# Seven block products of 512 columns for the output product, and another order at four joints of a trunk layer

## The chip, the cores and the metric

One NeuronCore of one Trainium2 chip runs the whole layer in one launch. The metric is the device time of an execution in microseconds (us); of several runs the median counts. The engines are named as in the profile: PE (TensorE, matmuls; PEld its weight loads), DVE (VectorE), ACT (ScalarE), POOL (GpSimd), SP (SyncE, which here only issues DMAs).

## What is computed

One layer of a decoder trunk with 512 tokens of 2048 channels, and 256 memory tokens. The input is normalised and projected onto 17408 columns: queries, keys, values and gates of three branches (block-sparse attention A with 8 heads, dilated windows B with 3 groups of 4 heads, cross-attention M into the memory with 4 heads) and three merge gates of 2048 columns.

```python
def reference(x, mem, norm_in_g, norm_mem_g, w_in, w_mem_kv, w_proj_a, w_proj_b, w_proj_m, w_out, norm_final_g):
    mem_n = rms_norm(mem, norm_mem_g)
    h = rms_norm(x, norm_in_g[layer])
    proj = jnp.einsum('bsd,de->bse', h, w_in[layer])
    (qa, ka, va, za, qb, kb, vb, zb, qm, zm, gates) = jnp.split(proj, split_points, axis=-1)
    ...
    mkv = jnp.einsum('bmd,de->bme', mem_n, w_mem_kv[layer])
    mk, mv = jnp.split(mkv, 2, axis=-1)
    ...
    g_a, g_b, g_m = jnp.split(jax.nn.sigmoid(gates), N_BRANCH, axis=-1)
    merged = (g_a * jnp.einsum('bse,ed->bsd', ya, w_proj_a[layer])
              + g_b * jnp.einsum('bse,ed->bsd', yb, w_proj_b[layer])
              + g_m * jnp.einsum('bse,ed->bsd', ym, w_proj_m[layer]))
    x = x + jnp.einsum('bsd,de->bse', merged, w_out[layer])
    return rms_norm(x, norm_final_g)
```

Everything is in float32 outside. Inside, each operand of a large product is cut into two parts, hi (rounded) and lo (the rest), and a product is three matmuls: hi x hi, hi x lo, lo x hi. ACT makes hi, DVE then lo = raw - hi. Each cut thus costs one instruction on either engine, and PE waits for both.

## The kernel before

Every engine takes its instructions in the order in which they stand in its queue; the order comes from the order of the code (a scheduler adds the semaphores). Weights come as pieces of 128 x 1024 through SP's queue; `load_half` (L67 to 79) cuts one into `whi` and `wlo`, of which three buffers each are kept. Four PSUM banks are called `acc`, four `att`.

- **Start, 5.9 to 79.6 us.** The first six columns of the gate path Z of branch M, with matmuls 512 tokens wide. Meanwhile `Rows.cut` (`mrows`) cuts the memory rows into `thi`, `tlo`, adding the squares on POOL (L207), and `normalize` (L275) scales the rows of x.
- **Memory keys, 79.6 to 136 us** (the loop over `h` and `c`, L320 to 330). Eight units K0 to K7, each a `project` of 16 x 3 matmuls of 256 columns (L97 to 99), which needs two cuts of weights; DVE then takes `mk` out of the bank (L327). After each two units `forms(h)` makes the forms of one pair of rows of x: sums and differences of the four 256-column blocks (L301 to 304), each then split into hi and lo (L149, L150): `u` (both T1 and T2), `halft` (T3), and the rows themselves into `kept`.
- **Memory values, 136 to 179.5 us.** `product_rows` (L102) with matmuls of 512 columns (L117 to 119); ACT takes `mv` out (L124). Four more forms are made here, two after each half.
- **Input products, from 179.5 us on.** A `Pair` of two 128-column units is computed by seven block products instead of eight (`steps`, L392 on; matmuls L360 to 362 of 256 columns) with weight sums on DVE (L397, L402, L415). Between them stand the attention of the branches, and `project_branch` (L598), the projection of a branch (its results leave from 375 to 450 us for M, 834 to 908 for A, 1358 to 1398 for B), which first splits all rows y of the branch. A list `later` holds small jobs, of which `run` pops one after each step.
- **The class table** of branch B's masks (`cls`, L713 to 719) is made on POOL at 909.6 us, transposed by PE (L717) and read back as `rowc`.
- **Gates, to 1839.8 us.** Eight triples of pairs; `projected` rows are loaded again (`pj`, through SP's queue) and DVE makes `merged` (L880, L882). Twelve of sixteen merged rows are spilled to DRAM and come back as `mg`.
- **Output product, 1839.8 to 2014.1 us.** `product_out` (L905 to 907): four column blocks of 512, four token blocks, 16 row blocks, three matmuls of 512 columns each. `cut_out` cuts the weights (`shi`, `slo`, L149, L150), DVE adds the residual (L924), ACT squares, POOL multiplies by the final gain (L928).
- **End, 2014.1 to 2023.1 us.** Scale of the last rows and stores.

`split` is in all of these places the same two instructions:

```python
nc.scalar.activation(hi, t, AF.Copy)
nc.vector.tensor_tensor(lo, t, hi.bitcast(F32), op=OP.subtract)
```

## Time and profile before

| | us |
|---|---|
| three runs | 2023.8, 2024.47, 2024.96 |
| median | 2024.47 |
| the profiled execution | 2024.92 |
| its span, first to last instruction | 2023.1 |
| PE busy | 1989.4 (98%) |
| DVE busy | 1466.7 (72%) |
| ACT busy | 988.0 (49%) |
| POOL busy | 124.1 (6%) |

The busy time of an engine counts every moment in which one of its instructions is under way; matmuls overlap, so the mean length of one is longer than the spacing of two. Windows give these per stretch, together with PEclk, the granted clock of PE (1.00 is 2.4 GHz, 0.50 is 1.2 GHz). A wait names the instruction that stood, and the one that released it. In the timeline, instructions of the same kind in a row are one line; the next start is the end of their spacing.

### The profile page before, as it was taken

How to read it: one execution, taken by the hardware profiler on the slowest of the kernel's cores; microseconds unless marked ns; L12 is line 12 of the kernel's file. 1: busy time of each engine (PE TensorE's matmuls, PEld its weight loads, DVE VectorE, ACT ScalarE, POOL GpSimd, SP SyncE). 2: the span in 40 equal slices, each digit the busy share in tenths (PEclk: the TensorE clock that was granted, in tenths of full speed). 3: DMA queues.
4: the chain of work that ended last, by engine and by line, in shares of the span. 5: the costliest groups of instructions: out<-in, count | busy, mean ns of one | idle time of the engine just before them, and what ended most of it. 6: DMA issues, size and time to landing. Idle time of an engine off the chain costs nothing.

```text
span 2023.1 us, 34915 instructions
## 1 busy us (share of the span) xinstructions
PE 1989.4 (98%) x14337; PEld 1886.9 (93%) x14337; DVE 1466.7 (72%) x1844; ACT 988.0 (49%) x1556; POOL 124.1 (6%) x179
## 2 busy tenths in 40 slices
PE   8999999999999999899999999999999999999998
PEld 6898999889999999789999999998999999998886
DVE  7977778338888888437887979855787878786233
ACT  6545565336555555323646454554444444445223
POOL 4200010010000000010000000001000000000110
PEclk9899999999999999999999999999999999999999
DMA  7464344433223223333322332345444444437332
GB/s 236 160 204 156 114 137 143 149 110 110 91 98 105 98 96 129 132 125 101 89 99 95 109 94 87 113 132 183 138 144 140 143 142 129 162 120 270 105 104 83
DMA packets 87600, 261.87 MB, mean 129 GB/s; under 512 B 15504, under 2 KB 16528, under 8 KB 87440
## 3 DMA queue, kind: packets, MB, share of 16 engines
q1 hardware_dynamic: 77376, 227.12, 33.9%
q0 software_dynamic: 9920, 32.51, 4.7%
q8 instruction: 112, 1.84, 0.4%
q14 instruction: 48, 0.39, 0.1%
q10 hardware_dynamic: 144, 0.02, 0.0%
HBM read 232.31 MB, written 27.30 MB: 128 GB/s over the span
## 4 chain that ended last, share of the span: by engine, by line
PE 54%; POOL 0%; ACT 0%; DVE 0%; ACTq 0%; issue 0%
PE acc L362 14%; PE acc L361 14%; PE acc L360 14%; PE acc L906 3%; PE acc L905 3%; PE acc L907 3%; PE acc L98 1%; PE acc L97 1%; PE acc L99 1%; PE att L822 1%; PE att L757 0%; PE att L811 0%; PE att L621 0%; PE att L762 0%; POOL combs L711 0%; PE att L760 0%
## 5 line engine op out<-in xcount | busy, mean ns | idle before, releaser
L350 ACT ACTIVATE whi<-raw 128x1024 fp32r<-128x1024 f32 x455 | 482.6, 1061 | 591.6 <-PE acc L361 396.1
L351 DVE TENSOR_TENSOR wlo<-raw,whi 128x1024 fp32r<-128x1024 f32 x455 | 555.8, 1222 | 199.2 <-ACT whi L350 189.0
L360 PE MATMUL acc<-kept,whi 128*128 128x256 f32 x2080 | 591.2, 284 | 0.6 <-ACT whi L350 0.3
L361 PE MATMUL acc<-kept,whi 128*128 128x256 f32 x2080 | 589.4, 283 | 0.4 <-DVE kept L150 0.4
L362 PE MATMUL acc<-kept,wlo 128*128 128x256 f32 x2080 | 589.1, 283 | 0.0
L360 PEld LDWEIGHTS acc<-kept,whi 128*128 128x128 f32 x2080 | 399.3, 192 | 1.6 <-ACT kept L149 0.7
L361 PEld LDWEIGHTS acc<-kept,whi 128*128 128x128 f32 x2080 | 399.5, 192 | 1.1 <-DVE kept L150 0.8
L362 PEld LDWEIGHTS acc<-kept,wlo 128*128 128x128 f32 x2080 | 399.3, 192 | 0.0
L360 PE MATMUL acc<-shi,whi 128*128 128x256 f32 x1040 | 296.7, 285 | 2.5 <-ACT shi L149 2.0
L361 PE MATMUL acc<-slo,whi 128*128 128x256 f32 x1040 | 296.4, 285 | 0.4 <-DVE slo L150 0.4
L362 PE MATMUL acc<-shi,wlo 128*128 128x256 f32 x1040 | 296.4, 285 | 0.0
L360 PEld LDWEIGHTS acc<-shi,whi 128*128 128x128 f32 x1040 | 201.5, 194 | 3.4 <-ACT shi L149 2.2
L361 PEld LDWEIGHTS acc<-slo,whi 128*128 128x128 f32 x1040 | 201.3, 194 | 1.0 <-DVE slo L150 0.6
L362 PEld LDWEIGHTS acc<-shi,wlo 128*128 128x128 f32 x1040 | 201.3, 194 | 0.2 <-DVE wlo L351 0.2
L78 DVE TENSOR_TENSOR wlo<-raw,whi 128x1024 fp32r<-128x1024 f32 x78 | 96.5, 1237 | 143.2 <-ACT whi L77 139.2
L77 ACT ACTIVATE whi<-raw 128x1024 fp32r<-128x1024 f32 x78 | 82.6, 1059 | 168.5 <-PE acc L98 126.1
L360 PE MATMUL acc<-T,whi 128*128 128x256 f32 x520 | 147.4, 283 | 0.0
L362 PE MATMUL acc<-T,wlo 128*128 128x256 f32 x520 | 147.2, 283 | 0.0
L361 PE MATMUL acc<-T,whi 128*128 128x256 f32 x520 | 147.2, 283 | 0.0
L98 PE MATMUL acc<-slo,whi 128*128 128x512 f32 x320 | 125.1, 391 | 4.3 <-DVE slo L150 4.3
L99 PE MATMUL acc<-shi,wlo 128*128 128x512 f32 x320 | 124.8, 391 | 0.0
L97 PE MATMUL acc<-shi,whi 128*128 128x512 f32 x320 | 121.4, 392 | 1.8 <-ACT shi L149 1.8
(244 smaller groups left out, 3199.3 us busy)
## 6 DMA issues: line engine op xcount, KB each, us to landing
raw<-in_w_in SPq DMA_DIRECT2D x266, 512.0 KB, 3.7
raw<-in_w_mem SPq DMA_DIRECT2D x32, 512.0 KB, 4.4
raw<-in_w_out SPq DMA_DIRECT2D x32, 512.0 KB, 6.1
projected<-pr POOLq DMA_DIRECT2D x48, 256.0 KB, 2.6
pj<-projected SPq DMA_DIRECT2D x48, 256.0 KB, 5.5
raw<-in_w_pm SPq DMA_DIRECT2D x16, 512.0 KB, 4.0
raw<-in_w_pa SPq DMA_DIRECT2D x16, 512.0 KB, 4.3
traw<-in_xT SPq DMA_DIRECT2D x16, 256.0 KB, 5.9
```

What stands on the lines that cost most here:

```text
L77: nc.scalar.activation(hi, raw, AF.Copy)
L78: nc.vector.tensor_tensor(lo, raw, hi.bitcast(F32), op=OP.subtract)
L97: nc.tensor.matmul(ps, whi, hi[i], start=i == 0, stop=False)
L98: nc.tensor.matmul(ps, whi, lo[i], start=False, stop=False)
L99: nc.tensor.matmul(ps, wlo, hi[i], start=False, stop=i == n - 1)
L350: nc.scalar.activation(hi, raw, AF.Copy)
L351: nc.vector.tensor_tensor(lo, raw, hi.bitcast(F32), op=OP.subtract)
L360: nc.tensor.matmul(ps, hi[:, sl], f[0], start=start and k == 0, stop=False, skip_group_check=True)
L361: nc.tensor.matmul(ps, hi[:, sl], f[1], start=False, stop=False, skip_group_check=True)
L362: nc.tensor.matmul(ps, lo[:, sl], f[0], start=False, stop=stop and k == 7, skip_group_check=True)
L905: nc.tensor.matmul(b, hi[:, sl], whi, start=k == 0, stop=False)
L906: nc.tensor.matmul(b, hi[:, sl], wlo, start=False, stop=False)
```

## The change

1. **Output product by seven block products.** Tokens are halved (2 x 256), the 2048 inputs are halved (8 row pairs), and two column blocks of 512 make a column pair. Per column pair seven products (forms B11, T1, T2, B21, T3, B22, T4 of the merged rows with sums of weight pieces) of four pieces each with 12 matmuls of 512 columns. `prepare` cuts a piece (`parts_1024`, `wlo` at L375 of the changed kernel) and makes its sums (`add_to`, L953).
2. **Forms of the merged rows** are made in the gate stage (`merged_forms`), T1 and T2 kept on the chip, the others spilled to `waiting` and fetched through POOL's queue by jobs in `later`. `pj` and the residual rows come through POOL's queue too.
3. **Order.** The class table's transpose moves to the start. The memory rows are cut before `silu_rows`. `forms` is called after each key unit but the first, and once in the middle of the values. The splits of y go to `later` before a projection. `turn_b` comes after `flush`.
4. **Memory.** 25 instead of 49 tiles of 512 columns (`slot`), 18 instead of 6 of 1024 (`raw`); T1/T2, T3 and the rows of x lie in the latter.

```diff
-SLOTS = 49
-RAWS = 6
+SLOTS = 25
+RAWS = 18
@@ at the start
+    clsT = att_bank()
+    nc.tensor.transpose(clsT[:, :P], classes(), ident)
+    rowc = sb.tile([P, 1], F32, name="rowc")
+    nc.vector.tensor_copy(rowc, clsT[:, 0:1])
@@ first units
-    for c in range(8):
+    for c in range(4):
         mrows.load()
     for i in range(EARLY):
         if i >= FIRST:
             first.append(project(w_in[U_ZM + i], hT))
-        nc.gpsimd.dma_start(zdram[i], silu_rows(first[i]))
-        if i >= FIRST:
             for c in range(3 if i < EARLY - 1 else 2):
                 mrows.cut()
+                if len(mrows.raw) < 8:
+                    mrows.load()
             for k in range(*((0, 5), (5, 11), (11, NK))[i - FIRST]):
                 normalize(k)
+        nc.gpsimd.dma_start(zdram[i], silu_rows(first[i]))
@@ memory keys and values
             nc.vector.tensor_tensor(t[:, c * MEM:(c + 1) * MEM], ps, mrow, op=OP.mult)
+            if h or c:
+                forms(2 * h + c - 1)
         nc.gpsimd.dma_start(mkd[h], t)
-        forms(h)
     for g in range(2):
...
-        forms(4 + 2 * g)
-        forms(5 + 2 * g)
+        if g == 0:
+            forms(7)
@@ Pair.run
-                if next(self.todo, None) and later:
-                    later.pop(0)()
+                at = next(self.todo, None)
+                if at:
+                    for _ in range(-(-len(later) // (8 - at))):
+                        later.pop(0)()
@@ before each project_branch, and in it
+    def act_later(y):
+        parts, tiles = [], [f() for f in y[:2]]
+        def one():
+            n = len(parts)
+            if n + 2 < len(y):
+                tiles.append(y[n + 2]())
+            parts.append(split(tiles[n]))
+        later.extend([one] * len(y))
+        return parts
...
-        act = tuple(zip(*[split(t()) for t in y]))
+        act = tuple(zip(*y))
...
+            if later:
+                later.pop(0)()
@@ gates
-                pr = slot("pj")
-                nc.sync.dma_start(pr, projected[b * NK + dt])
+            prs = [fetched(projected[b * NK + dt], "pj") for dt in pair]
...
+        merged_forms(i)
@@ output product, per column pair cp
+    def prepare(n):
+        if n < len(work) and n not in ready:
+            f, i = work[n]
+            raw = f(i)
+            raw, after = raw if isinstance(raw, tuple) else (raw, None)
+            if n < len(work) - 4:
+                ready[n] = parts_1024(raw)
+            else:
+                ready[n] = split(raw, (wide_tile("last", F32R), wide_tile("last", F32R)))
+            if after:
+                after()
+
+    def multiply(banks, n, form, start, stop, tiles=(0, 1), pieces=range(4)):
+        for i in pieces:
+            prepare(n + i + 1)
+            if n + i < len(work) - 8:
+                prepare(n + i + 2)
+            hi, lo = ready[n + i]
+            for t in tiles:
+                for kk in range(2):
+                    f = M[form][2 * i + kk]
+                    fh, fl = (p[:, t * P:(t + 1) * P] for p in f)
+                    wh, wl = (p[:, kk * 512:(kk + 1) * 512] for p in (hi, lo))
...
+                    nc.tensor.matmul(banks[t], fh, wh, start=first, stop=False, skip_group_check=True)
+                    nc.tensor.matmul(banks[t], fh, wl, start=False, stop=False, skip_group_check=True)
+                    nc.tensor.matmul(banks[t], fl, wh, start=False, stop=last, skip_group_check=True)
+            if later:
+                later.pop(0)()
...
+        multiply(xs, n, "B11", True, False)
+        for t in range(2):
+            add_block(t, c1, xs[t], OP.add)
+            residual(2 + t, c2)
+        multiply(ys, n + 4, "T1", True, False)
...
+        multiply(xs, n + 8, "T2", False, False)
...
+        multiply(zs, n + 12, "B21", True, True)
+        for t in range(2):
+            add_block(t, c1, zs[t], OP.add)
+            gained(t, c1)
...
+        multiply(xs, n + 16, "T3", False, False)
...
+        multiply(ys, n + 20, "B22", False, True)
...
+            multiply(xs, n + 24, "T4", False, True)
```

What the change does to the queues is seen best in the order of the instructions. First DVE's queue in the memory keys, around the end of K2, before (`slo`, `T`, `kept` are lo parts of the forms):

```order
L78 TENSOR_TENSOR wlo<-raw,whi 128x1024
L327 TENSOR_TENSOR mk<-acc,mrow 128x256
L301 TENSOR_TENSOR u<-traw 128x256
L78 TENSOR_TENSOR wlo<-raw,whi 128x1024
L303 SCALAR_TENSOR_TENSOR u<-u,traw 128x256
L304 SCALAR_TENSOR_TENSOR traw<-u,traw 128x256
L78 TENSOR_TENSOR wlo<-raw,whi 128x1024
L150 TENSOR_TENSOR slo<-u,shi 128x512
L150 TENSOR_TENSOR T_1070<-halft,T_1070 128x256
L327 TENSOR_TENSOR mk<-acc,mrow 128x256
L150 TENSOR_TENSOR kept_75<-traw,kept_75 128x512
L78 TENSOR_TENSOR wlo<-raw,whi 128x1024
```

And in the changed kernel, from the weights of K3 and K4 to those of K5 and K6:

```order
L91 TENSOR_TENSOR wlo<-raw,whi 128x1024 x4
L350 TENSOR_TENSOR mk<-acc,mrow 128x256 x2
L321 TENSOR_TENSOR u<-xraw 128x256 x2
L323 SCALAR_TENSOR_TENSOR u<-u,xraw 128x256 x2
L324 SCALAR_TENSOR_TENSOR xraw<-u,xraw 128x256 x2
L163 TENSOR_TENSOR T_1157<-u,T_1157 128x512
L163 TENSOR_TENSOR kept_83<-xraw,kept_83 128x512
L163 TENSOR_TENSOR kept_84<-xraw,kept_84 128x512
L163 TENSOR_TENSOR T_1234<-u,T_1234 128x512
L163 TENSOR_TENSOR T_1237<-halft,T_1237 128x256 x2
L91 TENSOR_TENSOR wlo<-raw,whi 128x1024 x4
```

Each `mk` reads the bank of its unit, as before (the two of `x2` are those of K3 and K4); the instructions of two forms now stand between the second `mk` and the next `wlo`, those of K5, in one block, where before a few stood between single `wlo`, and one `wlo` of the next unit or two stood ahead of each `mk`.

The second place is ACT's queue in the memory values, where the first half ends, before:

```order
L149 ACTIVATE kept_77<-traw 128x512
L77 ACTIVATE whi<-raw 128x1024 x8
L124 ACTIVATE mv<-acc,mcol 128x512
L77 ACTIVATE whi<-raw 128x1024
L124 ACTIVATE mv<-acc,mcol 128x512
L77 ACTIVATE whi<-raw 128x1024
L149 ACTIVATE shi<-u 128x512
```

And changed:

```order
L162 ACTIVATE T_1391<-u 128x512
L162 ACTIVATE T_1394<-halft 128x256 x2
L90 ACTIVATE whi<-raw 128x1024 x10
L137 ACTIVATE mv<-acc,mcol 128x512 x2
L162 ACTIVATE T_1560<-u 128x512
L162 ACTIVATE kept_87<-xraw 128x512
L90 ACTIVATE whi<-raw 128x1024 x8
```

The second `mv` had a `whi` ahead of and behind it; now two hi parts stand between it and the next eight `whi`.

The third place is DVE's queue in the output product. Before, from the last merged rows on, all cuts of a column block stand in a row (`x16`, 512 columns):

```order
L150 TENSOR_TENSOR kept_86<-mg,kept_86 128x512
L150 TENSOR_TENSOR kept_87<-mg,kept_87 128x512
L924 TENSOR_TENSOR res<-acc,res 128x512 x4
L150 TENSOR_TENSOR slo<-raw,shi 128x512 x16
L924 TENSOR_TENSOR res<-acc,res 128x512 x4
L150 TENSOR_TENSOR slo<-raw,shi 128x512 x16
```

Changed, around the end of the fourth of the seven products in the first column pair (`raw<-raw` are sums of weight pieces, `T` and `kept` are forms that came back from DRAM, `att` is the bank of the fourth product):

```order
L1030 TENSOR_TENSOR res<-res,acc 128x512 x2
L375 TENSOR_TENSOR wlo<-raw,whi 128x1024
L953 TENSOR_TENSOR raw<-raw 128x1024
L163 TENSOR_TENSOR T_20603<-mg,T_20603 128x256
L375 TENSOR_TENSOR wlo<-raw,whi 128x1024
L953 TENSOR_TENSOR raw<-raw 128x1024
L163 TENSOR_TENSOR T_20603<-mg,T_20603 128x256
L953 TENSOR_TENSOR raw<-raw 128x1024
L1030 TENSOR_TENSOR res<-res,att 128x512
L375 TENSOR_TENSOR wlo<-raw,whi 128x1024
L163 TENSOR_TENSOR T_20650<-mg,T_20650 128x256
L1030 TENSOR_TENSOR res<-res,att 128x512
```

A `res<-res,att`, which reads a bank that PE has to finish, now stands between the cuts of the pieces, among sums and splits of 256 columns.

## Rows read from the trace of the kernel before

**Rows 1.** The page's busy times, their share of the span, and the instructions.
```profile
PE 1989.4 (98%) x14337; PEld 1886.9 (93%) x14337; DVE 1466.7 (72%) x1844; ACT 988.0 (49%) x1556; POOL 124.1 (6%) x179
```

**Rows 2.** Windows, key stage, output product, end: length, busy (count) per engine, PEclk, DMA, GB/s.
```profile
101.40:136.00 34.60, 34.60 (x291) 34.60 (x290) 28.82 (x48) 18.34 (x24) 1.64 (x3) 1.00 0.63 204
1839.80:2014.10 174.30, 174.28 (x770) 143.97 (x768) 65.54 (x118) 55.69 (x112) 18.59 (x18) 1.00 0.37 132
2014.10:2023.10 9.00, 0.00 (x0) 0.00 (x0) 2.69 (x8) 2.26 (x5) 0.00 (x0) 0.78 0.49 178
```

**Rows 3.** Windows, the four joints.
```profile
79.60:101.40 21.80, 17.92 (x109) 16.92 (x108) 17.34 (x30) 10.12 (x16) 3.97 (x3) 0.77 0.33 111
179.50:200.00 20.50, 17.09 (x104) 15.41 (x103) 14.64 (x20) 9.09 (x15) 1.08 (x2) 0.83 0.39 134
810.70:825.00 14.30, 8.18 (x29) 6.26 (x29) 11.11 (x16) 5.71 (x10) 1.10 (x2) 0.76 0.35 112
909.60:920.00 10.40, 8.29 (x57) 8.09 (x56) 3.44 (x8) 3.37 (x6) 2.38 (x9) 0.84 0.31 101
```

**Rows 4.** Waits of PE: total us, times, the longest.
```profile
PE acc L98 <- DVE slo L150: 4.3, 1, 4.3
PE acc L98 <- DVE tlo L198: 3.7, 2, 3.0
PE att L717 <- POOL cls L714: 2.1, 1, 2.1
PE acc L360 <- ACT shi L149: 2.0, 1, 2.0
```

**Rows 5.** Windows, the stretches at a low clock within the joints.
```profile
87.20:97.40 10.20, 9.33 (x40) 8.74 (x41) 8.00 (x15) 5.28 (x8) 3.41 (x2) 0.50 0.51 179
189.50:196.40 6.90, 6.60 (x30) 6.12 (x30) 3.24 (x4) 2.55 (x4) 0.00 (x0) 0.51 0.37 123
814.20:821.00 6.80, 3.34 (x8) 2.66 (x9) 5.74 (x9) 1.40 (x4) 0.55 (x1) 0.50 0.59 191
913.20:916.60 3.40, 3.40 (x18) 3.40 (x18) 1.34 (x5) 1.25 (x2) 0.00 (x0) 0.51 0.48 152
```

**Rows 6.** Timeline of DVE, 81 to 110 us: start, us, operation, xcount.
```profile
81.27 3.69 DVE L150 TENSOR_TENSOR kept<-traw,kept 128x512 fp32r<-128x512 f32 x6
...
101.54 0.75 DVE L327 TENSOR_TENSOR mk<-acc,mrow 128x256 f32<-128x256 f32 x2
...
106.97 1.22 DVE L78 TENSOR_TENSOR wlo<-raw,whi 128x1024 fp32r<-128x1024 f32 x1
108.10 0.42 DVE L327 TENSOR_TENSOR mk<-acc,mrow 128x256 f32<-128x256 f32 x1
```

**Rows 7.** Timelines of DVE and of POOL, 63 to 69 us.
```profile
63.89 0.87 DVE L198 SCALAR_TENSOR_TENSOR tlo<-traw,gains_sb,thi 128x256 fp32r<-128x256 f32 x2
...
65.82 2.95 DVE L198 SCALAR_TENSOR_TENSOR tlo<-traw,gains_sb,thi 128x256 fp32r<-128x256 f32 x2
...
64.96 3.52 POOL L207 TENSOR_TENSOR sq<-sq 128x512 f32<-128x512 f32 x2 [4.73 <-ACT sq L203]
```

**Rows 8.** Groups by form, DVE in the output product, POOL of the whole.
```profile
L150 DVE TENSOR_TENSOR slo<-raw,shi 128x512 fp32r<-128x512 f32 x60 | 40.0, 718 | 24.0 <-ACT shi L149 14.1 <-PE acc L906 9.2 <-issue 0.4
L924 DVE TENSOR_TENSOR res<-acc,res 128x512 f32<-128x512 f32 x15 | 10.4, 692 | 74.4 <-PE acc L907 74.4
L150 DVE TENSOR_TENSOR kept<-mg,kept 128x512 fp32r<-128x512 f32 x8 | 5.2, 683 | 0.0
...
L928 POOL TENSOR_TENSOR res<-res,gf 128x512 f32<-128x512 f32 x12 | 15.5, 1293 | 106.3 <-ACT sq L926 106.3
```

**Rows 9.** Groups by form, ACT, 101.4 to 179.5 us.
```profile
L77 ACT ACTIVATE whi<-raw 128x1024 fp32r<-128x1024 f32 x26 | 27.5, 1058 | 31.4 <-PE acc L119 14.3 <-PE acc L98 11.6 <-issue 4.5
L149 ACT ACTIVATE shi<-u 128x512 fp32r<-128x512 f32 x6 | 3.8, 630 | 2.7 <-DVE u L303 2.5
...
L124 ACT ACTIVATE mv<-acc,mcol 128x512 f32<-128x512 f32 x3 | 2.1, 690 | 3.6 <-PE acc L119 3.6
```

More of the change, by code (lines that the diff above doesn't have):

```diff
@@ L841, in trunk_layer @@
             gates[0][1].run()
-    project_branch(2, yB, w_pb, first_w)
+            flush()
+    project_branch(2, actB, w_pb, first_w)
     merged = [None] * NK
-    parts_of = [None] * NK
-    spill = dram.tile([NK, P, 512], F32, name="spill")
-    pieces = {}
-    def cut_out(u):
-        if u < 16 and u not in pieces:
-            pieces[u] = []
-            for half in range(2):
-                raw = sb.tile([P, 1024], F32, name="raw", bufs=RAWS)
-                nc.sync.dma_start(raw, w_out[u][:, half * 1024:(half + 1) * 1024])
-                pieces[u] += [split(raw[:, c * 512:(c + 1) * 512]) for c in range(2)]
@@ new lines, in fetch_then, with fetch, ahead_by, piece @@
+    def fetch_then(src, shape, use):
+        got = []
+        def fetch():
+            t = slot("mg")[:, :shape]
+            nc.gpsimd.dma_start(t, src)
+            got.append(t)
+        return fetch, lambda: use(got[0])
+    def ahead_by(n, jobs):
+        fetches, uses = zip(*jobs)
+        def piece(i):
+            def run():
+                for f in fetches[0 if i == 0 else i + n:i + n + 1]:
+                    f()
+                uses[i]()
+            return run
+        return [piece(i) for i in range(len(jobs))]
@@ new lines, in piece, with add_to, prepared, p1 @@
+    def piece(c, i):
+        raw = wide_tile("raw")
+        nc.sync.dma_start(raw, w_out[4 * c + i // 2][:, i % 2 * 1024:(i % 2 + 1) * 1024])
+        return raw
+    def add_to(a, b):
+        nc.vector.tensor_tensor(a, a, b, op=OP.add)
+        return a
+    parts = sb.tile([P, 4, 4], F32, name="parts")
+    early = sb.tile([P, 4], F32, name="early")
+    rows_done = dram.tile([4, 2, P, 512], F32, name="rows_done")
+    gf, rs = {}, {}
+    def prepared(c1, c2):
+        a11, s = {}, {}
+        def p1(i):
+            a11[i] = piece(c1, i)
+            return a11[i]
+        def p5(i):
+            s[i] = add_to(piece(c2, i), piece(c2, 4 + i))
+            return s[i]
+        def p6(i):
+            return add_to(s[i], a11[i])
+        def p2(i):
+            a12 = piece(c1, 4 + i)
+            return a12, lambda: add_to(s[i], a12)
+        def q7(i):
+            return add_to(a11[i], piece(c2, i))
+        def q3(i):
+            return s[i]
+        def p4(i):
+            return piece(c2, 4 + i)
+        return [(f, i) for f in (p1, p5, p6, p2, q7, q3, p4) for i in range(4)]
@@ new lines, in finish_row @@
+    def finish_row(t, c):
+        squares_of(t, c)
+        r = rstd(parts[:, t, c:c + 1], early[:, t:t + 1])
+        rows = slice(t * P, (t + 1) * P)
+        for n_, c_ in enumerate([b for b in range(4) if b != c][:2] + [c] + [b for b in range(4) if b != c][2:]):
+            y = rs[t, c_]
+            if c_ == c:
+                nc.vector.scalar_tensor_tensor(y, y, r, gf[1][:, c % 2 * 512:(c % 2 + 1) * 512], op0=OP.mult,
+                                               op1=OP.mult)
+            elif n_ == 0:
+                nc.vector.tensor_scalar(y, y, r, None, op0=OP.mult)
+            else:
+                nc.scalar.activation(y, y, AF.Copy, scale=r)
+            nc.sync.dma_start(out[rows, c_ * 512:(c_ + 1) * 512], y)
@@ L864, in trunk_layer, with early_sum @@
+    def early_sum(t, c):
+        nc.vector.tensor_reduce(early[:, t:t + 1], parts[:, t, :2], axis=AX.X, op=OP.add)
+        nc.vector.tensor_tensor(early[:, t:t + 1], early[:, t:t + 1], parts[:, t, 5 - c:6 - c], op=OP.add)
+        nc.vector.tensor_scalar(early[:, t:t + 1], early[:, t:t + 1], 1.0 / D, EPS, op0=OP.mult, op1=OP.add)
     for i in range(8):
@@ L866, in trunk_layer @@
         for n, b in enumerate((0, 1, 2)):
-            prs = []
-            for dt in pair:
-                pr = slot("pj")
-                nc.sync.dma_start(pr, projected[b * NK + dt])
-                prs.append(pr)
-            done = gates[i][n].run(6)
-            if i == 7 and n == 1:
-                for dt in range(4):
-                    parts_merged(dt)
+            prs = [fetched(projected[b * NK + dt], "pj") for dt in pair]
+            done = gates[i][n]
             if i == 7 and n == 2:
-                cut_out(0)
+                done.run(2)
+                later.extend(ahead_by(2, [left(k, "B11") for k in range(7)]))
+                done.run(4)
+                prepare(0)
             done.run()
@@ L884, in trunk_layer @@
                     merged[dt] = g
-        if i < 8 - HELD // 2:
-            for dt in pair:
-                nc.gpsimd.dma_start(spill[dt], merged[dt])
-                merged[dt] = None
-    def product_out(n, last):
-        banks = [acc_bank() for _ in whole]
-        for group in [[u] for u in range(4 - last)] + [list(range(4 - last, 4))]:
-            for u in group:
-                cut_out(4 * n + u)
-                if n == 0 and u:
-                    for dt in range(4 * u, 4 * u + 4):
-                        parts_merged(dt, kept[dt])
-            cut_out(4 * n + group[-1] + 1)
-            for b, sl in zip(banks, whole):
-                for k in [4 * u + kk for u in group for kk in range(4)]:
-                    (hi, lo), (whi, wlo) = parts_of[k], pieces[4 * n + k // 4][k % 4]
-                    nc.tensor.matmul(b, hi[:, sl], whi, start=k == 0, stop=False)
-                    nc.tensor.matmul(b, hi[:, sl], wlo, start=False, stop=False)
-                    nc.tensor.matmul(b, lo[:, sl], whi, start=False, stop=k == NK - 1)
-        return banks
```

186 lines of the change are left out of this document (126 added, 60 removed).

## The prediction

> **What bounds the kernel now.** The page's busy times come first: TensorE (PE) is busy 98% of the span [rows 1], so time goes only where PE loses it or has fewer matmuls. Then the windows give the price of a matmul. In the output product 770 matmuls, 768 of them of 512 columns, take 174.3 us with PE busy all through, 0.227 each; in the key stage of the memory 288 of 256 columns fill 34.6 us, 0.120 each [rows 2]. The means of 283 to 391 ns in other views are latencies that overlap, so I use the spacings. With these, the windows at the four joints show the loss [rows 3]:
>
> - 79.6 to 101.4: 109 instructions at no more than 0.120 are 13.1, so 8.7 of 21.8 us are lost.
> - 179.5 to 200: 104 x 0.120 = 12.5, so 8.0 of 20.5 lost.
> - 810.7 to 825: 29 x 0.227 = 6.6, so 7.7 of 14.3 lost.
> - 909.6 to 920: a wait of 2.1 [rows 4] and 3.4 us at half clock [rows 5], which cost 1.7: 3.8.
>
> The waits of PE name what came late there: lo parts on VectorE (tlo 3.7, slo 4.3), a hi part on ScalarE (shi 2.0), the class table on GpSimd (2.1) [rows 4]. Behind each such wait the granted clock is 0.50 or 0.51, the 1.2 GHz level, for 3.4 to 10.2 us [rows 5], and half of PE's busy time in them (9.33, 6.60, 3.34, 3.40) is what that costs: 4.7, 3.3, 1.7, 1.7, or 2.8 on the mean. So a gap of PE costs more than its length.
>
> **The output product.** 4 x 16 x 4 x 3 = 768 matmuls become 2 x 7 x 4 x 12 = 672: 96 x 0.227 = **-21.8 us**. Its price is VectorE. Before, it worked 65.5 of these 174.3 us [rows 2]. Now each column pair cuts 28 weight pieces (1024 columns: VectorE 1.14 us of spacing, from 106.97 to 108.10 [rows 6]) and makes 16 sums (1.14 each, the same shape). The first pair also cuts the forms of the merged rows that come back from DRAM. Its queue up to the piece that the 18th group of 12 matmuls needs holds 17 cuts (19.4), 14 sums (16.0), 21 instructions of 512 columns (0.615 each, six in 3.69 [rows 6]: 12.9) and 15 of 256 columns (0.36 each, two in 0.75 [rows 6]: 5.4). That is 53.7 us, of which 2.9 lie before the product: done at 50.8. PE would want that piece after 17 groups of 12 x 0.227, at 46.5. So it waits 4.3 there; and as shown in the rows of the order, a residual sum that waits for PE's fourth product stands ahead of a cut, which makes up to 6.5. I take **+5.5** (0 to 8; 0 if the queue starts further ahead than the last product's end). At the change of column pairs the first banks are used again once the last residual sum (0.69 [rows 8]) has read them: **+0.9** (0 to 2). These waits of 2 to 4 us are as long as those that halved the clock [rows 4], but each must be followed by such a stretch for it: 0 to 5, **+1.7**, the smallest price seen.
>
> GpSimd multiplies the finished rows by the gain beside this, 1.29 us each [rows 8]. What it does to VectorE: two cuts of tlo took 0.87 us alone and 2.95 beside GpSimd's sums, two in 3.52 [rows 7], about 1 us lost for each; but 60 cuts of slo in the output product, beside 12 multiplications, took 718 ns on the mean where the cuts of the merged rows, ahead of them, took 683: 60 x 0.035 = 2.1 in all, 0.18 each [rows 7, 8]. Some four fall where VectorE is late: 0.7 to 4, and I take the middle, **+2.0**. The Trainium skill (SBUF — State Buffer, "SBUF: two separate sides") has a rule against this change: a VectorE instruction with two SBUF operands and a GpSimd one that reads SBUF hold a shared pair of ports in turn, each for its whole length. By it the term would be 4 x 1.29 = 5.2; the pair of tlo agrees with it more than the 60 cuts do.
>
> The output product thus gains -21.8 + 5.5 + 0.9 + 1.7 + 2.0 = **-11.7** (-18 to -4). The last stretch of 9.0 us without matmuls [rows 2] has the same steps: 0 (-1 to 1).
>
> **The key stage of the memory.** The forms of x were cut in small pieces between the weight cuts; now two whole forms (four splits each pair of rows) stand in one block. VectorE takes its queue in order. The block stands behind mk, which waits for the end of a unit, and ahead of the first cut wlo of the next unit. PE can do two matmuls of that unit (0.24) and then stands. Before, one or two cuts of the next unit were ahead of each mk. With 256 columns at 0.37, 512 at 0.615, a weight cut at 1.14 [rows 6]:
>
> - after K1: mk, four of 256 and two of 512, cut: 5 x 0.37 + 2 x 0.615 + 1.14 = 4.2, less 0.24: 4.0
> - after K2: mk, ten of 256, four of 512, cut: 7.7, less 0.24: 7.4
> - after K4, and after K6: mk, eight of 256, four of 512, cut: 6.9, less 0.24: 6.7 each
> - middle of the values V: the same on ScalarE, where mv (0.69, read as its length) and two hi parts (0.63 long, some 0.52 apart) stand ahead of whi (1.06) [rows 9], then the cut 1.14: 3.9, less one matmul 0.23: 3.7.
>
> Sum **+28.5**. The lower end is 0: over K2 to K7 VectorE has 12 x 1.14 + 7 x 0.37 + 6 forms of 3.1 = 34.9 us of work for 34.6 us of PE [rows 2], so with another order it would hardly cost. I take the upper end, since the order is fixed and each engine's queue is in order. Five gaps as long as those that halved the clock, or longer, add 5 x 2.5 (0 to 5 x 4.7) = **+12.5**; a little under the mean of 2.8, since VectorE works ahead while PE is slow.
>
> **The joints.** In K0 and K1 the cuts of the memory rows come earlier but VectorE still has six splits and the units' cuts before the scale chain; I give back **-3** of the 8.7 lost (0 to -6). The start of the first seven-product pair has its forms done: **-8.0** (-8.5 to -5). Project A's rows are split ahead through `later`: **-7.7** (-8 to -4). The class table leaves the path: **-3.8** (-4 to -3); what it takes at the start lies beside the loads of x. The 48 pj loads move from SP's to GpSimd's queue, past no weight load any more, and GpSimd issues 12 spills and some 20 fetches more than before, on an engine that is busy 6% [rows 1]; a load that came late there would hold a product of g on VectorE, which is covered: 0 (0 to 2). The merged forms in the gate stage add some 2 us of VectorE for three pairs, 72% busy over all [rows 1]: 0, and if that cover fell short in the last pairs, 2.
>
> **Sum.** -11.7 + 28.5 + 12.5 - 3 - 8.0 - 7.7 - 3.8 = **+6.8**. The profiled execution took 2024.9, 0.5 above the median of the runs, so the median goes from 2024.5 to about **2031**.
>
> **The rivals.**
>
> - VectorE's queue runs ahead in the key stage, because mk comes out early enough or the blocks are shorter than their rows: no gaps, no half clock there, -41 against my sum, **1990**: faster. It decides where mk's block ends before PE's unit does. For it: PE there had no wait before. Against: mk cannot run before its unit ends. Chance 0.12.
> - The gaps come but the clock stays at full: -12.5 - 1.7, **2017**, from which a few us of the gaps decide the sign. For it: only four gaps of the trace show what follows. Against: all of these show it. Chance 0.15 (0.10 faster, 0.05 the same).
> - The clock stays half over all of K2 to K7: 34.6 lost in place of 12.5, **2053**: 0.06. Against it: PE in the first joint was back at full clock within 10.2 us.
> - GpSimd shuts VectorE out for each whole multiplication, and eight of them fall where it is late: 8 x 1.29 = 10.3 in place of 2.0, **2039**: 0.07. This is the case of the Trainium skill's page named above.
> - A joint's loss stays, since the early splits in `later` run out of time: +8, **2039**: 0.05.
>
> **How the numbers follow.** My forecast (2024 to 2038) gets 0.55, of it 0.13 below 2028.5. A measurement of this kernel tells about 0.2%, 4 us, from no change. Faster: 0.12 + 0.10 = 0.22. Same: 0.13 + 0.05 = 0.18. Slower: 0.42 + 0.06 + 0.07 + 0.05 = 0.60. The range leaves out the first rival, a part of the second and the third: 2016 to 2043.
>
> **What would show it.** In the profile after: 672 output matmuls in some 152 to 165 us; waits of PE for wlo of 4 to 7 us after K1, K2, K4 and K6 and one of about 4 in the values, with PEclk near 0.5 behind them; a key stage from 101 to 136 that has become some 60 us long; no wait for cls, and none over 1 us for shi or slo at 180 and 810. I am wrong if PE shows no wait for wlo in the key stage, if its clock stays at 1.0 behind them, or if the output product waits for nothing (then it gains 21.8) or for over 15 us.

## The result: 2058 us, and where the time went

| | before | after |
|---|---|---|
| median of the runs | 2024.72 (4 runs, 2023.8 to 2025.53) | 2058.11 (4 runs, 2054.07 to 2062.22) |
| ratio, 95% interval | | 1.0165, 1.0138 to 1.0192 |
| the profiled execution | 2024.92 | 2054.51 |
| its span | 2023.1 | 2052.7 |

The kernel became slower, as forecast, but by 33 us and not by 7, and outside the range (2016 to 2043). The four runs fall into two pairs, at 2054 and at 2062 us, and the profiled execution is of the lower one; what follows adds up to its 29.6 us.

The page's busy times of the kernel after answer to [rows 1]:

```profile
PE 1983.7 (97%) x14241; PEld 1870.4 (91%) x14241; DVE 1556.1 (76%) x1940; ACT 1018.8 (50%) x1572; POOL 199.2 (10%) x291
```

PE has 96 matmuls less and is busy 5.7 us less, and yet the span is 29.6 longer: the time is lost in waits and at half clock. First the windows, by stage, of the kernel after (length, busy us with counts for PE, PEld, DVE, ACT, POOL, then PEclk, DMA share, GB/s): the first units, K0 and K1, K2 to K7, the values, the gates, the output product.

```profile
6.20:86.80 80.60, 74.30 (x306) 56.99 (x306) 72.76 (x91) 52.89 (x90) 41.53 (x26) 0.98 0.61 211
86.80:102.80 16.00, 13.18 (x110) 12.69 (x108) 14.14 (x30) 7.59 (x13) 5.05 (x4) 1.00 0.18 66
102.80:166.30 63.50, 43.78 (x289) 42.08 (x290) 34.72 (x59) 21.31 (x31) 1.08 (x2) 0.81 0.35 117
166.30:214.90 48.60, 45.32 (x195) 35.73 (x193) 23.62 (x24) 19.72 (x21) 2.16 (x4) 1.00 0.58 190
1414.70:1865.60 450.90, 445.02 (x3697) 443.79 (x3696) 367.54 (x424) 214.87 (x300) 41.18 (x76) 1.00 0.44 151
1865.60:2043.90 178.30, 163.41 (x674) 129.31 (x673) 146.56 (x180) 83.02 (x121) 53.78 (x71) 0.95 0.60 203
```

Two of these stages were not shown of the kernel before; here they are, the first units and the gates:

```profile
5.90:79.60 73.70, 72.47 (x305) 56.62 (x305) 68.11 (x82) 48.74 (x82) 33.53 (x25) 1.00 0.66 224
1396.00:1839.80 443.80, 443.77 (x3697) 443.55 (x3696) 357.53 (x390) 210.44 (x294) 10.53 (x20) 1.00 0.44 147
```

With [rows 2, 3] this gives the differences of the table; the remaining stages, and the tenths of all, are taken from the starts of the same matmuls in both traces.

| stage | before | after | difference | predicted |
|---|---|---|---|---|
| first units, to K0 | 73.7 | 80.5 | +6.9 | 0 |
| K0, K1 and the wait behind | 21.8 | 16.0 | -5.8 | +3.5 (4.0 + 2.5 - 3) |
| K2 to K7 | 34.6 | 63.5 | +28.9 | +28.3 (20.8 + 7.5) |
| values | 43.6 | 48.6 | +5.1 | +6.2 (3.7 + 2.5) |
| input products of M and A, project A | 726.6 | 713.0 | -13.7 | -15.7 (8.0 + 7.7) |
| class table and branch B | 446.0 | 442.1 | -4.0 | -3.8 |
| project B | 43.8 | 44.8 | +1.0 | 0 |
| gates | 443.8 | 450.9 | +7.1 | 0 |
| output product | 174.3 | 178.2 | +4.0 | -11.7 |
| end, and the first matmul's start | 15.0 | 15.1 | +0.2 | 0 |
| sum | | | **+29.6** | **+6.8** |

PE's waits of the kernel after, where before stood [rows 4]:

```profile
PE acc L110 <- ACT whi L90: 19.0, 4, 5.5
PE acc L1019 <- ACT whi L374: 10.5, 4, 4.2
...
PE acc L112 <- DVE wlo L91: 5.9, 5, 2.6
PE acc L384 <- DVE g L454: 5.9, 7, 1.1
PE acc L1020 <- DVE wlo L375: 4.1, 5, 1.7
PE acc L130 <- ACT whi L90: 2.8, 1, 2.8
```

The four waits for shi, slo, tlo and cls are gone; in their place stand 19.0 us for whi in the key stage (L110), 10.5 and 4.1 in the output product (L1019, L1020) and seven waits of about 1 us in the gates (L384).

**The key stage** has the gaps that were walked, with another last link. DVE after the end of K2 (start, us, engine, line, operation):

```profile
111.75 0.42 DVE L350 TENSOR_TENSOR mk<-acc,mrow 128x256 f32<-128x256 f32 x1 [6.17 <-PE acc L112]
112.09 0.75 DVE L321 TENSOR_TENSOR u<-xraw 128x256 f32<-128x256 f32 x2
...
117.85 3.48 DVE L91 TENSOR_TENSOR wlo<-raw,whi 128x1024 fp32r<-128x1024 f32 x3
```

ACT and PE at the same time:

```profile
113.21 0.63 ACT L162 ACTIVATE T<-u 128x512 fp32r<-128x512 f32 x1 [9.54 <-DVE u L323]
...
116.07 2.93 ACT L90 ACTIVATE whi<-raw 128x1024 fp32r<-128x1024 f32 x3
```

```profile
117.17 0.58 PE L110 MATMUL acc<-thi,whi 128*128 128x256 f32 x1 [5.45 <-ACT whi L90]
```

`mk` waits for the end of K2 and starts at 111.75; the block of two forms runs until 117.85, when the cut of K3's weights begins. On ACT the hi parts of the forms wait for DVE (9.54), and `whi` for K3 comes behind them at 116.07. PE stands for 5.45 us, starts at 117.17 and, after two matmuls, stands 1.16 more for `wlo`. The prediction had PE stand for `wlo` on DVE alone, with `whi` ready; most of the wait is for `whi` on ACT, which stood behind the same forms. The sum is nearly the same, 6.6 us against 7.4. This returns after K4 and K6. Behind each of the three waits the clock is at its 1.2 GHz level for 6.8 us; the first:

```profile
115.60:122.40 6.80, 4.07 (x17) 3.78 (x18) 5.74 (x9) 3.41 (x5) 0.00 (x0) 0.50 0.39 130
```

**The output product** lost 25.7 us against 672 matmuls at 0.227 (152.5): 14.6 of it in the waits above, and the clock was at half for 17 us of it (PEclk 0.95 on the mean). ACT and POOL around its longest wait, 4.2 us at 1919 to 1923:

```profile
1917.59 0.42 ACT L162 ACTIVATE T<-mg 128x256 fp32r<-128x256 f32 x1 [2.81 <-DMA mg<-waiting]
1921.89 0.42 ACT L162 ACTIVATE T<-mg 128x256 fp32r<-128x256 f32 x1 [3.88 <-DMA mg<-waiting]
1922.21 1.04 ACT L374 ACTIVATE whi<-raw 128x1024 fp32r<-128x1024 f32 x1
```

```profile
1913.00 0.55 POOL L913 DMA_DIRECT2D mg<-waiting  x1 [2.04 <-DVE T L163]
1918.76 0.55 POOL L913 DMA_DIRECT2D mg<-waiting  x1 [5.22 <-DVE T L163]
```

ACT stands on a fetch (`DMA mg<-waiting`) at 1917.59 and again at 1921.89, 2.81 and 3.88 us, and the cut `whi` of 1922.21, for which PE waits, is behind it in the queue. The fetches are not ahead: POOL issues each of these only when DVE has cut the form of the fetch before (`<-DVE T L163`, 2.04 and 5.22 us), and it takes 3 to 5 us from issue to the cut. Of the 25 tiles of 512 columns, T1 and T2 hold 16 and the residual rows up to 8.

**The gates** wait in each group for one result. DVE there, and the window ahead of it:

```profile
1449.06 1.23 DVE L423 TENSOR_TENSOR raw<-raw 128x1024 f32<-128x1024 f32 x1 [3.10 <-DMA raw<-in_w_in]
...
1452.80 0.41 DVE L454 SCALAR_TENSOR_TENSOR g<-acc,hd 128x256 f32<-128x256 f32 x1
```

```profile
1446.00:1449.00 3.00, 3.00 (x27) 3.00 (x26) 0.00 (x0) 1.06 (x1) 0.00 (x0) 1.00 1.01 381
```

DVE is idle for 3.10 us until a weight has landed; then it is late with `g` (L454), which PE needs. In the 3 us before, the transfers are full (share 1.01, 381 GB/s). POOL has just issued six loads of pj within 5 us, beside three spills; the last three:

```profile
1443.98 1.63 POOL L478 DMA_DIRECT2D pj<-projected  x3 [0.45 <-PE acc L386]
```

### The profile page after: what moved, and what is told of

It is laid out like the page before. It is cut to its first block, busy times and chain, and to the rows that moved or that the text cites. A ratio compares the mean times of both kernels' runs of the same rounds, so it can differ in the third digit from the quotient of the medians.

```text
span 2052.7 us, 34930 instructions
## 1 busy us (share of the span) xinstructions
PE 1983.7 (97%) x14241; PEld 1870.4 (91%) x14241; DVE 1556.1 (76%) x1940; ACT 1018.8 (50%) x1572; POOL 199.2 (10%) x291
## 5 line engine op out<-in xcount | busy, mean ns | idle before, releaser
L374 ACT ACTIVATE whi<-raw 128x1024 fp32r<-128x1024 f32 x507 | 537.2, 1060 | 611.8 <-PE acc L385 376.9
L375 DVE TENSOR_TENSOR wlo<-raw,whi 128x1024 fp32r<-128x1024 f32 x507 | 622.8, 1229 | 178.3 <-ACT whi L374 167.9
L384 PE MATMUL acc<-kept,whi 128*128 128x256 f32 x2080 | 591.3, 284 | 6.0 <-DVE g L454 5.9
L384 PE MATMUL acc<-T,whi 128*128 128x256 f32 x1560 | 442.2, 283 | 0.5 <-ACT ha L430 0.5
L385 PE MATMUL acc<-T,whi 128*128 128x256 f32 x1560 | 441.6, 283 | 0.0
L386 PE MATMUL acc<-T,wlo 128*128 128x256 f32 x1560 | 441.6, 283 | 0.0
L384 PEld LDWEIGHTS acc<-kept,whi 128*128 128x128 f32 x2080 | 399.0, 192 | 7.9 <-issue 7.1
L384 PEld LDWEIGHTS acc<-T,whi 128*128 128x128 f32 x1560 | 299.3, 192 | 1.1 <-ACT ha L430 0.7
L385 PEld LDWEIGHTS acc<-T,whi 128*128 128x128 f32 x1560 | 299.4, 192 | 0.3
L386 PEld LDWEIGHTS acc<-T,wlo 128*128 128x128 f32 x1560 | 299.3, 192 | 0.0
L91 DVE TENSOR_TENSOR wlo<-raw,whi 128x1024 fp32r<-128x1024 f32 x78 | 95.7, 1236 | 149.5 <-ACT whi L90 149.5
L90 ACT ACTIVATE whi<-raw 128x1024 fp32r<-128x1024 f32 x78 | 81.6, 1056 | 167.7 <-PE acc L111 118.1
L110 PE MATMUL acc<-shi,whi 128*128 128x512 f32 x320 | 126.7, 396 | 0.5 <-ACT pr L137 0.5
L423 DVE TENSOR_TENSOR raw<-raw 128x1024 f32<-128x1024 f32 x65 | 79.5, 1223 | 22.4 <-DMA raw<-in_w_in 20.7
L441 DVE TENSOR_TENSOR raw<-raw 128x1024 f32<-128x1024 f32 x65 | 79.4, 1221 | 0.9
L428 DVE TENSOR_TENSOR raw<-raw 128x1024 f32<-128x1024 f32 x65 | 79.3, 1221 | 0.9
```

Of the source, the lines that this page charges most:

```text
L90: nc.scalar.activation(hi, raw, AF.Copy)
L91: nc.vector.tensor_tensor(lo, raw, hi.bitcast(F32), op=OP.subtract)
L110: nc.tensor.matmul(ps, whi, hi[i], start=i == 0, stop=False)
L374: nc.scalar.activation(hi, raw, AF.Copy)
L375: nc.vector.tensor_tensor(lo, raw, hi.bitcast(F32), op=OP.subtract)
L384: nc.tensor.matmul(ps, hi[:, sl], f[0], start=start and k == 0, stop=False, skip_group_check=True)
```

## The experiments

The stage's window stands under each. All kernels but the last three ran once, so what one execution differs from another must be kept in mind: in the changed kernel and the four whose edits don't touch the output product, this took 177.6 to 179.5 us, while the stretch up to the end of the values was 4 to 5 us longer in two executions whose edits don't touch it (pj on SP's queue, and the fetches through SP's queue). The matmuls of the output product alone are 152.5 us.

**Weights cut ahead in the key stage.** `load_unit` of all sixteen units is made first, and the next one is cut before the result is taken out:

```diff
-            ps = project(w_mem[2 * h + c], mT, MEM)
+            ps = project(None, mT, MEM, cuts[2 * h + c])
+            for half in range(2):
+                cuts[2 * h + c + 1](half * 1024, P)
```

> In the key stage and in the middle of the values the weights of the next unit are cut (in the order of the code) ahead of the product's result mk or mv and of the forms; nothing else is changed. Theory A (the loss of 33.9 us from the second key unit's end to the first input product is the order alone): waits of about 1.5 us are left behind two or three units, and with their half clock the loss goes down to 5 to 12. Rival B (VectorE has as much work there as PE, 34.9 to 34.6 us, and is late in any order): at least 20 stay.

Measured 2023.95 us, a single run. K2 to K7, then the values:

```profile
100.20:138.50 38.30, 34.59 (x290) 33.96 (x289) 34.22 (x65) 21.34 (x34) 1.62 (x3) 1.00 0.47 156
138.50:184.80 46.30, 45.20 (x195) 36.13 (x195) 25.82 (x27) 20.89 (x22) 2.16 (x4) 1.00 0.65 222
```

The loss from K2 to the end of the values is 6.4 us in place of 34.0. DVE does the same instructions in 34.22 us of the 38.30. So the order alone had cost it, and the joint behind still has its forms ready. Theory A holds; the kernel is back at the time of before.

**The forms of x at their old places in the code.**

```diff
-            if h or c:
-                forms(2 * h + c - 1)
         nc.gpsimd.dma_start(mkd[h], t)
+        forms(h)
...
-        if g == 0:
-            forms(7)
+        forms(4 + 2 * g)
+        forms(5 + 2 * g)
```

> The changed kernel with the forms of x called where the kernel before calls them (after each two key units, and after both halves of the values). Theory A (one block of two forms behind mk is what costs 33.9 us from the second unit's end on): one form stands there now, some 3 us of VectorE in place of 6 to 7, and twice no form: 10 to 18 us are lost up to the first input product; the joint at its start loses about 8 again. Rival B (what changed is not the forms' place but the memory tiles or the loads): still over 28 lost before the first input product.

Measured 2042.71 us. K2 to K7, then the values:

```profile
102.70:141.30 38.60, 35.95 (x288) 35.55 (x289) 26.63 (x39) 16.91 (x21) 1.08 (x2) 0.96 0.55 182
141.30:197.50 56.20, 46.81 (x194) 36.78 (x192) 28.71 (x41) 23.59 (x31) 3.25 (x6) 0.96 0.46 157
```

K2 to K7 lose 4.0, but the values 12.6 where they had lost nothing before, and the stretch behind them 3.0 more than in the changed kernel, not 8. The 16.6 us lie in the range of theory A, but their place does not: the old calls don't give the old queue. I had described the queue's order as that of the code, with a scheduler that only adds semaphores; it also moves instructions, as the `wlo` among the forms of one call in the queue of before show, and here DVE has the two forms of the values in one block again. What moves them otherwise than before (the tiles are other ones) was not tried, so a part of rival B stays open for these 16.6 us.

**pj on SP's queue.**

```diff
-            prs = [fetched(projected[b * NK + dt], "pj") for dt in pair]
+            prs = []
+            for dt in pair:
+                pr = slot("pj")
+                nc.sync.dma_start(pr, projected[b * NK + dt])
+                prs.append(pr)
```

> The projected rows (pj) are loaded through SP's queue again, as before the change. Theory A (GpSimd's queue, which no weight load holds back, issues six of these loads in a row beside the spills, and the transfers delay the weights of the next pair): the seven waits of about 1 us of PE in the gate stage go, and the stage from 451.1 to about 444. Rival B (VectorE's work on the merged forms makes its results late): they stay, within 2 us of 451.

Its first execution took 2404.53 us, at a granted clock of 0.75 from end to end, and says nothing on the question. The second:

> The same kernel as in the run before it with pj on SP's queue, whose profile shows a granted clock of 0.75 over the whole execution and says nothing on the question. Theory A: the waits of about 1 us in the gate stage go, the stage from 451 to about 444. Rival B: they stay, within 2 us of 451.

Measured 2051.13 us. The gates:

```profile
1419.20:1862.90 443.70, 443.70 (x3697) 443.53 (x3696) 367.72 (x424) 214.92 (x300) 15.78 (x29) 1.00 0.46 153
```

443.7 us, as before, and no wait for `g` is left. DVE does all its work on the merged forms in this time (367.7 us), so that was covered, as predicted. Theory A holds. The total fell by only 3.4, since in this execution K0 to the values lost 6.2 us more (1.3 of it in waits, the rest in longer stretches at half clock), and the first units 1.6 less.

**silu_rows ahead of the cuts of the memory rows.**

```diff
+        nc.gpsimd.dma_start(zdram[i], silu_rows(first[i]))
+        if i >= FIRST:
             for c in range(3 if i < EARLY - 1 else 2):
                 mrows.cut()
...
-        nc.gpsimd.dma_start(zdram[i], silu_rows(first[i]))
```

> In the units 3 to 5 the result is taken out (silu_rows) ahead of the cuts of the memory rows again. Theory A (the wait of 2.6 us at 71.7 and the half clock behind it come from this order): the first key unit starts at 82 to 84 in place of 86.8, but the first two key units, which took 16.0 us, take 19 to 22, since the cuts are late again. Rival B (the first stage is late for other reasons, VectorE beside GpSimd's sums): it still starts within 1 us of 86.8.

Measured 2057.92 us. The first units, then K0 and K1:

```profile
6.00:82.10 76.10, 72.35 (x305) 55.84 (x306) 68.40 (x83) 48.64 (x82) 33.88 (x25) 1.00 0.65 225
82.10:106.30 24.20, 16.45 (x110) 15.43 (x108) 19.38 (x39) 10.91 (x20) 4.51 (x4) 0.86 0.12 44
```

The first units gain 4.5, and K0 with K1 lose 8.2: theory A by its start (82.1), but 24.2 us for the two key units are more than the 19 to 22 expected. So the new order is worth 3.7 us in all. Of the 6.9 us in the first units 2.4 stay. They lie in the first three units, where PE waits 2.4 us for lo parts of x and 1.3 for those of weights, 0.7 and 0.5 in the kernel before; DVE has these cuts in another order there. That was not tried further.

**Fetches without a tile.** The fetch goes straight into the lo half of the form's own tile and is cut there:

```diff
-            t = slot("mg")[:, :shape]
-            nc.gpsimd.dma_start(t, src)
-            got.append(t)
+            got.append(parts())
+            nc.gpsimd.dma_start(got[0][1].bitcast(F32), src)
...
+            nc.scalar.activation(hi, lo.bitcast(F32), AF.Copy)
+            nc.vector.tensor_tensor(lo, lo.bitcast(F32), hi.bitcast(F32), op=OP.subtract)
```

> The spilled forms of the merged rows are fetched straight into the lo half of the tile that will hold their parts, and cut there, so that no fetch needs one of the 25 tiles of 512 columns. Theory A (of these tiles 16 hold T1 and T2 and up to 8 the residual rows, so that a fetch waits for the cut of the form before it, and ScalarE stands on the fetch ahead of the cuts of the weights): PE loses 25.8 us in the output product of the changed kernel; here at most 10, and the output product goes from 178 us to 155 to 163. Rival B (VectorE has too much to do in this product, whatever the fetches do): it stays within 5 us of 178.

Measured 2050.54 us. The output product:

```profile
1868.00:2039.90 171.90, 161.01 (x674) 127.30 (x672) 144.94 (x179) 82.82 (x121) 54.29 (x63) 0.98 0.60 210
```

171.9: 6.3 less, between A and B. Nothing holds the fetches back now, and they come as a burst: for the first 15 us the share of the transfers is 1.03, and ACT stands on the fetches. The second 5 us of the product, in which PE works 2.28, and ACT ahead of a `whi` a little later:

```profile
1873.00:1878.00 5.00, 2.28 (x9) 1.36 (x8) 4.10 (x8) 4.25 (x7) 1.79 (x5) 0.99 1.03 393
1881.58 0.42 ACT L917 ACTIVATE T<-T 128x256 fp32r<-128x256 f32 x1 [2.83 <-DMA T<-waiting]
```

**The same through SP's queue**, fetches and residual rows, so that the weight loads pace them:

```diff
-            nc.gpsimd.dma_start(got[0][1].bitcast(F32), src)
+            nc.sync.dma_start(got[0][1].bitcast(F32), src)
...
-        nc.gpsimd.dma_start(rs[t, c], x[t * P:(t + 1) * P, c * 512:(c + 1) * 512])
+        nc.sync.dma_start(rs[t, c], x[t * P:(t + 1) * P, c * 512:(c + 1) * 512])
```

> As the run with fetches straight into the lo half (171.9 us in the output product), but these fetches and the residual rows go through SP's queue, among the loads of the weight pieces. Theory A (what was left in that run comes from a burst: 20 fetches issued in 20 us fill the transfer engines, share 1.03, and ScalarE stands on the fetches ahead of weight cuts): the output product goes to 158 to 166. Rival B (VectorE's amount of work is what is left): within 3 us of 172.

Measured 2041.85 us. The output product:

```profile
1867.50:2031.00 163.50, 156.21 (x674) 125.16 (x672) 144.14 (x180) 82.01 (x121) 36.96 (x31) 1.00 0.65 223
```

163.5, another 8.4 less, the clock at 1.00. Theory A holds for both: 14.7 of the 25.7 us lost came from how the fetches, and with them the residual rows, were issued; what the residual rows alone did is not shown. What is left is 11.0, and PE waits in it for nothing but `wlo`:

```profile
PE acc L1025 <- DVE wlo L375: 7.2, 5, 3.4
```

**No fetches, no cuts of B21, B22, T3 and T4:**

```diff
-    later.extend(ahead_by(2, [right(k) for k in range(8)] + [third_form(k) for k in range(8)]
-                          + [left(k, "T4") for k in range(8)]))
+    for k in range(8):
+        M["T3"][k] = T["T3"][k]
```

> The forms B21, B22, T3 and T4 of the merged rows are neither fetched nor cut in the output product (old parts of x are multiplied in their place); the rest is as in the changed kernel. Theory A (the fetches and what they hold up are the whole unexpected loss): the output product falls from 178.2 to 153 to 158, with 152.5 the time of the matmuls alone. Rival B (weight cuts and sums of VectorE, or the weight loads, are a limit too): over 163.

Measured 2036.0 us. The output product:

```profile
1865.80:2025.30 159.50, 156.06 (x674) 126.99 (x672) 135.31 (x157) 73.58 (x98) 38.75 (x47) 0.99 0.58 201
```

159.5, between the two: 7 us are lost even without any form that is fetched. PE waits for `wlo` there (3.4 us in two waits), with 3.4 us of half clock behind the longer one. So weight cuts and sums, with POOL's multiplications beside them, are a limit too.

**No multiplications by the gain on POOL:**

```diff
-        nc.gpsimd.tensor_tensor(rs[t, c], rs[t, c], gf[c // 2][:, c % 2 * 512:(c % 2 + 1) * 512], op=OP.mult)
```

> GpSimd's multiplications by the final gain are left out (the rows are not multiplied there). Theory A (each holds VectorE up by 0.2 us, as read in the kernel before): the output product gets at most 2 us shorter. Rival B (each shuts VectorE out for up to 1.3 us where it is late): 5 to 10 us shorter.

Measured 2051.7 us. The output product, then DVE's cuts in it, without and (second fence) with the multiplications of the changed kernel:

```profile
1867.20:2041.10 173.90, 161.61 (x674) 128.49 (x672) 137.39 (x182) 82.60 (x122) 32.05 (x59) 0.96 0.59 202
```

```profile
L375 DVE TENSOR_TENSOR wlo<-raw,whi 128x1024 fp32r<-128x1024 f32 x51 | 62.1, 1220 | 10.7 <-ACT whi L374 10.4
```

```profile
L375 DVE TENSOR_TENSOR wlo<-raw,whi 128x1024 fp32r<-128x1024 f32 x51 | 66.1, 1301 | 3.9 <-ACT whi L374 3.9
```

4.4 us less, between the two. 51 cuts at 1220 in place of 1301 ns, and 31 sums at 1218 in place of 1266, are 5.6 us of DVE. That is 0.5 on the mean of twelve multiplications, but it does not spread evenly, as the part on why the prediction was wrong shows.

**Three edits together:** weights ahead in the key stage; fetches in place; pj, fetches and residual rows on SP's queue (the fetches three ahead).

> Three edits together: the weights of the next key unit cut ahead of mk and the forms; pj, the fetches and the residual rows on SP's queue; the fetches straight into the lo half. By the stages of the single runs: key stage and values lose 6 in place of 34, gates 0 in place of 7, output product 164 in place of 178: 2054.5 - 28 - 7 - 15 = 2005 (2000 to 2010), 20 under the kernel before. If the edits share a cause: above 2015.

Measured 2003.35 us, ratio 0.9897 to before (0.9881 to 0.9914): 1% faster than the kernel before. K2 to K7 take 38.3 us and the values 46.2, as with the first edit alone. Gates and output product:

```profile
1384.70:1828.30 443.60, 443.60 (x3698) 443.56 (x3697) 368.59 (x425) 215.48 (x302) 11.88 (x22) 1.00 0.46 153
1828.30:1990.60 162.30, 156.69 (x673) 126.64 (x672) 143.89 (x179) 82.18 (x120) 37.69 (x31) 0.99 0.65 225
```

The three add up. Two attempts at more on top of it:

> The same with silu_rows ahead of the cuts of the memory rows in units 3 to 5, as before. By the single run the first units gain 4.5 and the first two key units lose 8: 3 to 4 slower than the kernel with three edits. Rival: with weights cut ahead the loss of the two key units does not come back, and it is 4 faster.

Measured 2006.86 us, 3.5 slower, as expected from the single run (its edit is the one shown above). The stages agree too: the first units take 76.1 us in place of 80.4, K0 with K1 21.9 in place of 13.7. The loss of the two key units comes back, and the rival is out.

> The same three edits, and GpSimd's multiplications of the first column pair moved into the second, where VectorE has slack. If each holds VectorE up by some 0.55 us, as the run without them showed (4.4 us for the eight of the first pair): 2 to 4 us faster than the kernel with three edits. If the loss only moves along: the same within 1 us.

```diff
+    def times_gain(t, c):
+        nc.gpsimd.tensor_tensor(rs[t, c], rs[t, c], gf[c // 2][:, c % 2 * 512:(c % 2 + 1) * 512], op=OP.mult)
...
                     rs[t, c] = fetched(rows_done[t, c], "res")
+                    times_gain(t, c)
```

Measured 2005.49 us, no gain, and neither of the two expectations: its four runs (2003.43 to 2007.71) overlap those of the kernel with three edits (2001.33 to 2004.33). The output product takes 166.9 us in place of 162.3, but here the trace of the longest of four executions stands against that of the shortest. The slack of DVE in the second pair, which I had estimated, did not take them up; why was not followed further.

## Why the prediction was wrong

The sign and most terms were right; the failure is in three places, which the table of stages separates.

1. **The output product, "-11.7".** The step "its price is VectorE" summed DVE's queue and took the fetched forms to be there when it came to them. They were not, and of the signs that I had named this one failed: 672 matmuls in 152 to 165 us (178.2). I had costed the fetches, on POOL's queue, by their busy time alone and never walked what a fetch waits for: a tile out of 25, with 16 and up to 8 in use. That chain, with ACT's queue behind it, and the burst that takes its place when the tiles are out of the way, cost 14.7 us by two runs (the residual rows moved along in the second). The terms I did write add up to 10.1 (5.5 + 0.9 + 1.7 + 2.0), and 11.0 is left without that chain, but the agreement is luck: the parts did not come. The 5.5 stood for a wait at the 18th group of twelve matmuls. The changed kernel has its longest wait just there, 4.2 us, but for ACT's `whi` behind a fetch; with the fetches through SP's queue 0.6 is left near it, at the 19th group, and the larger waits stand at the 7th (2.0) and the 27th (3.4). None stands at the change of column pairs (0.9), and the clock stayed at 1.00 (1.7). (The sum has a slip, too: 17 x 12 x 0.227 is 46.3 and not 46.5.)

   POOL's multiplications were mis-sized: 4.4 in the run without them, where I took 2.0 (range 0.7 to 4). I had read 0.18 each as a price; it is a mean over twelve, of which nine ran while DVE waited or had only small work of 0.15 us. Three met a cut `slo` and made it 0.68 us longer. One of these three, with two cuts in 1.97 us that take 1.3 otherwise:

```profile
1885.08 1.30 POOL L928 TENSOR_TENSOR res<-res,gf 128x512 f32<-128x512 f32 x1 [1.43 <-ACT sq L926]
1885.56 1.97 DVE L150 TENSOR_TENSOR slo<-raw,shi 128x512 fp32r<-128x512 f32 x2 [1.31 <-ACT shi L149]
```

   In the changed kernel DVE works 146.6 of the 178.3 us, and six of the eight multiplications of the first pair made a DVE instruction longer, by 0.35 to 1.5 us, 5.8 in all. The Trainium skill's rule (SBUF — State Buffer, "SBUF: two separate sides") would have given, as an estimate, 5.2 for four. The rows agree with it where a multiplication met an instruction with both operands in SBUF (most often about 1 us lost, of 1.29), and the mean hid that. The rival of eight whole multiplications, 10.3 us, did not come.
2. **The gates, "0 (0 to 2)".** The step said that pj moves "past no weight load any more" and counted this as nothing. That weight loads no longer hold pj back was the cost: six loads within 5 us delay a weight by 3 us, and PE by about 1 us in seven groups, 7.1 in all, and nothing with pj on SP's queue. The cover that I named, DVE's slack, held for DVE's own work.
3. **The first units, "0", and K0 with K1, "-3 of the 8.7".** The cuts moved ahead of silu_rows delay a `wlo` by 2.6 us and halve the clock there (4.5, by the run that undoes it), and give 8.2 in K0 and K1. I had priced only the second half, and too low. With 2.4 in the first three units, whose waits are named above and whose cause stays open, the errors of these two rows nearly cancel: +1.1 where +3.5 was forecast, by luck.

Right were the gaps of the key stage (20.8 walked and 7.5 for the clock in K2 to K7 against 28.9 measured, 19.7 of it waits), though PE stood mostly for `whi` where I had named `wlo`, the two joints (15.7 against 13.7) and the class table (3.8 against 4.0). The values agree in size (6.2 against 5.1) but only the wait came (3.3 us where 3.7 was walked); the clock stayed at 1.00 in this execution, where I had put 2.5, and 1.8 of the 5.1 have no name. The rival of a VectorE that runs ahead is refuted by the waits; that of a clock that stays high, or low all through, by the windows; that of a joint that stays, by the 13.7.

Open is why the median lies 3.6 us above the profiled execution. The run with pj on SP's queue lost 4.6 us more than that one up to the end of the values, with the same 19.7 us of waits from K2 to K7 but longer stretches at half clock: 10.2 us behind K2, K4 and K6, where it was 6.8, and one of 6.8 in the values. Behind K2:

```profile
114.80:125.00 10.20, 6.79 (x30) 6.50 (x31) 6.44 (x11) 5.15 (x8) 0.00 (x0) 0.50 0.46 154
```

Whether the untraced executions differ in this way is not shown.

## What to carry to other kernels

Before a prefetch is counted as hidden, list what holds its destination's buffer and what paces its queue: too few tiles make a chain of it, and a queue with nothing to pace it makes a burst. When a result that waits for PE is taken out on the engine that also cuts the next operands, cut these first. A block of work moved off one joint should be walked through every queue at the place where it lands, above all the one that it joins. A price that is a mean over many rows should be split into the rows that were hit and those that were not, since the change can alter their share.
